# Weight chunks split three chunks ahead with four buffers, and a planner that adds a margin behind each estimated landing

## The chip, the cores and the metric

The kernel runs on one core of a Trainium2 chip. Five engines work side by side, each through its own instructions in the order in which the program lists them: TensorE (PE), VectorE (DVE), ScalarE (ACT), GpSimd (POOL) and SyncE (SP, which here only issues transfers). The metric is the device time of one execution in microseconds; the time before is the median of three runs.

## What is computed

One inference step of a one-layer decoder trunk. A prompt of 512 tokens and 8 samples of 4 tokens (32 rows) share the weights, so the projection has 544 token rows of width 2048:

```python
h = rmsnorm(x, norm_in)
z = einsum('btd,dc->btc', h, w_in)          # 7712 columns
# group A, 8 heads: sparse attention (compressed, selected, window), 2 key/value heads
# group B, 8 heads: forgetting attention, logit += D[t] - D[s], D = cumsum(log f)
mix = concat(o_n * silu(z_n), o_f * silu(z_f))
y = rmsnorm(x + einsum('btc,cd->btd', mix, w_out), norm_final)
```

The samples read 1024 past tokens each out of paged caches (8 pages of 128 rows a sample, through a page table) and a window state of 512 rows. All of it is in float32. The kernel also returns the new key/value rows, the log forget values and the shifted window state.

## The kernel before, in words

**Weights.** The input projection is 61 tiles of up to 128 columns of `w_in`, each made over four chunks of 4 x 128 rows; the first tile is made in plain float32, the other 60 tiles (240 chunks) in two parts. A raw chunk (128 x 512 floats) is fetched by SP (`raw`), then split: ACT writes its rounded high part (`whi`), DVE the rest (`wlo`). A chunk is 24 matmuls of 272 columns: two token halves, four row blocks, and for each the three products high x high, high x low, low x high (`mm3`, output `pz`). `run_tiles` goes over tiles and chunks and, in the second token half of chunk m, calls `w_split(m + W_AHEAD, part)` for the two parts; `W_AHEAD` is 2, so `whi` and `wlo` have three buffers each. `w_split` also fetches the raw chunk that lies four behind the one it splits (`w_dma`); there are five raw buffers. The finished tile is scaled into `zt` and a `post` stream stores it or hands it on.

After the last tile `run_outputs` does the same with 64 chunks of `w_out` (output `po`); `ahead(m)` keeps its splits `W_AHEAD` in front.

**Streams.** Everything else is written as Python generators, the streams: the start, the page indices, the forgetting attention (`fox`, twice sample half then prompt half, four heads each), the sparse attention (`nsa`: compression, prompt, sample), and for each of the 16 heads `mix` (gate times attention) and `turn_in` (its split into the two parts `h_hi` and `h_lo` that the output projection reads). While `run_tiles` lists the projection's matmuls, it calls `S.pump()` after every three of them, which lets every stream go on that is due, and the stream's instructions land at that place in the program.

**The planner.** When a stream is due is decided while the program is built, by the class `Clock`. It keeps an estimated time for each engine, for each transfer, and for each buffer the end of its last write and last read. A stream can yield a list of tiles: then its next step is listed once PE's planned time has passed `Clock.ready(tile)`, the latest write or read of it plus `HOP`, 0.25 us. For a tile that a transfer fills, the write's end is the estimated landing. On the chip each instruction still waits on semaphores for what it truly needs; the planner decides only the order. If a transfer lands later than planned, the instruction that needs it waits, and all that is listed behind it on its engine waits too.

The loads that streams wait on: cache pages for the forgetting attention (`fpg`, four gathers or page loads of 256 KB to a page tile, two page tiles in flight, from POOL or SP), rows for the compression (`crow`, two in flight) and its weights (`cw`), sets of cache pages for the sparse sample part (`spg`, five in flight, 48 sets), and operands that went through memory between stages (`fz`, `nz`, `fvz`, `dsb`, `kvc`; for each key/value head of the sparse prompt two keys and four query heads, one after the other; `mx` and `oz` for each mixed head, four heads at a time).

Gate tiles that are finished before the sparse sample part has given back its memory are stored (`scr_m`) and loaded later (`mx`); the later ones are written in place. The output projection can begin only when the in-projection has read `h_hi` and `h_lo` for the last time, because `turn_in` overwrites them.

**Scratch.** `dynamic_dma_scratch_size` is the memory in each partition that is set aside for the descriptors of POOL's transfers, 8192 bytes.

Of the kernel before, what the change touches and what calls it, by code (L numbers as in the profile page):

```python
# [40 lines left out]
class Clock:  # L41

    HOP = 0.25

    def __init__(self):
        self.t = dict(pe=0.0, dve=0.0, act=0.0, pool=0.0, sp=0.0)
        self.gate, self.row = {}, {}
        self.lanes = {q: [0.0] * 8 for q in ("sp", "pool")}
        self.ring, self.bus = 0.0, {}
        self.slot, self.wr, self.rd, self.plane, self.parts = {}, {}, {}, {}, {}  # L50
        self.end = 0.0
        self.stall = {}
        self.who = ""
# [14 lines left out]
        return [(*k, i) for i in range(lo // step, hi // step + 1)]  # L68

    def ready(self, ap):  # L70
        return max(max(self.wr.get(k, (0.0, 0))[0], self.rd.get(k, (0.0, 0))[0]) for k in self.keys(ap)) + self.HOP

    def packet(self, aps):
        least = 4096
# [47 lines left out]
    def note(self, eng, op, a, k):  # L122
# [12 lines left out]
        for s in reads:  # L135
            w = self.wr.get(s) if s else None
            if w:
                start = max(start, w[0] + (self.HOP if w[1] != eng else 0.0))
        for s in filter(None, writes):
            for d in (self.wr, self.rd):  # L140
                w = d.get(s)
                if w and not ("dma" in op and w[1] == "dma"):
                    start = max(start, w[0] + (self.HOP if w[1] != eng else 0.0))
        dma = "dma" in op
# [19 lines left out]
        else:  # L164
            end = start + self.cost(eng, op, outs[0], aps, accum is not None)
            self.t[eng] = end
            self.end = max(self.end, end + self.HOP)
        for s in reads:
# [152 lines left out]
def trunk_step(ctx, tc, x_prompt, x_sample, cache_nsa_kv, cache_fox_kv, cache_fox_logf, state_nsa_win,  # L321
# [4 lines left out]
    nc = Engines(tc.nc, clock)  # L326
# [71 lines left out]
    def cp(out, in_, scale=1.0):  # L398
        nc.scalar.activation(out, in_, AF.Copy, scale=scale)

    def low(hi, lo, src, scale=None):
        if scale is None:
            nc.vector.tensor_tensor(lo, src, hi, op=OP.subtract)
        else:
            nc.vector.scalar_tensor_tensor(lo, src, scale, hi, op0=OP.mult, op1=OP.subtract)
# [8 lines left out]
    def mm3(out, a, b, start, stop):  # L414
        nc.tensor.matmul(out, a[0], b[0], start=start, stop=False, skip_group_check=True)
        nc.tensor.matmul(out, a[0], b[1], start=False, stop=False, skip_group_check=True)
        nc.tensor.matmul(out, a[1], b[0], start=False, stop=stop, skip_group_check=True)

    def mm(out, a, b, start=True, stop=True):
        nc.tensor.matmul(out, a, b, start=start, stop=stop, skip_group_check=True)  # L420
# [49 lines left out]
            if ch and k % 4 == 3:  # L470
                out_steps.append((4, 4 * (ch - 1) + k // 4))
    out_steps += [(3, i) for i in range(8)]
    W_RAW, W_AHEAD = 5, 2

    def out_steps_kind(m):
        j = m - 4 * n_in
# [33 lines left out]
    def w_split(m, part):  # L510
        t, c = divmod(m, 4)
        if t == 0 or m >= 4 * n_in + len(out_steps):
            return
        n = tiles[t]["m"] if t < n_in else P
        raw = raws[m][:, :, :n]
        if part == 0:
            if t >= n_in and out_steps[m - 4 * n_in][0] == 4:
                i = out_steps[m - 4 * n_in][1]
                if "w" not in last_w:
                    wl = MX["pl"].tile([P, 2, 16, 256], F32R, name="wl", tag="mx")  # L520
                    clock.parts[wl.tensor.name] = (2 * 16 * 256, 512)
                    last_w["w"] = wl
                wsp[m] = [last_w["w"][:, x, 2 * i:2 * i + 2, :].rearrange("p a b -> p (a b)").rearrange("p (a b) -> p a b", b=P)
                          for x in range(2)]
            else:
                wsp[m] = [wts.tile([P, 4, P], F32R, name=w, bufs=W_AHEAD + 1) for w in ("whi", "wlo")]
            cp(wsp[m][0][:, :, :n], raw)
        else:
            low(*(x[:, :, :n] for x in wsp[m]), raw)
            if t < n_in:  # L530
                del raws[m]
                if m > 4:
                    w_dma(m - 1 + W_RAW)

    def run_tiles(t0, t1):
        for t in range(t0, t1):
            spec = tiles[t]
            if t == 0:
                S.need("begun")
            if t - 2 >= 0:  # L540
                S.need(f"post{t - 2}")
            n = spec["m"]
            zt = stg.tile([P, TOK], F32, name="zt", bufs=2)
            tile_of[zt.tensor.name] = t
            clock.parts[zt.tensor.name] = (TOK, HALF)
            cuts = ((0, HALF), (HALF, TOK))
            ps = [psum.tile([P, b - a], F32, name="pz", tag="pz", bufs=2) for a, b in cuts]
            raw_part = []
            for c in range(4):
                m = t * 4 + c  # L550
                if t == 0:
                    S.need(*[f"x{k}" for k in range(4 * max(c, 1), 4 * max(c, 1) + 4)])
                    for hf, cut in enumerate(cuts):
                        sl = slice(*cut)
                        for b in (h_hi, h_lo):
                            for kk in range(4):
                                mm(ps[hf][kk * 32:kk * 32 + 32], w_0["w"][:, m * 4 + kk], b[:, c * 4 + kk, sl].bitcast(F32),
                                   c == 0 and b is h_hi, c == 3 and b is h_lo)
                            S.pump()
                    w_split(m + W_AHEAD, 0)  # L560
                    w_split(m + W_AHEAD, 1)
                    if c == 3:
                        for hf, cut in enumerate(cuts):
                            cp(zt[:, slice(*cut)], ps[hf])
                        flags.add("t0")
                    S.pump()
                    continue
                hi, lo = wsp.pop(m)
                for hf, cut in enumerate(cuts):
                    sl = slice(*cut)  # L570
                    for kk in range(4):
                        k = c * 4 + kk
                        mm3(ps[hf][:n], (hi[:, kk, :n], lo[:, kk, :n]), (h_hi[:, k, sl], h_lo[:, k, sl]),
                            c == 0 and kk == 0, c == 3 and kk == 3)
                        if kk == 3 and c == 3:

                            if t > 1:
                                S.need("rsb")
                            elif t == 1:
                                raw_part.append(sl)  # L580
                            late = max(clock.t["dve"], clock.t["pe"]) > max(clock.t["act"], clock.t["pe"]) + 0.2
                            if t == 1:
                                (cp if late else nc.vector.tensor_copy)(zt[:n, sl], ps[hf][:n])
                            elif late:
                                cp(zt[:n, sl], ps[hf][:n])
                                raw_part.append(sl)
                            else:
                                nc.vector.tensor_tensor(zt[:n, sl], ps[hf][:n], rsb[:n, sl], op=OP.mult)
                        if hf == len(cuts) - 1 and kk % 2 == 0:
                            w_split(m + W_AHEAD, kk // 2)  # L590
                        if hf == len(cuts) - 1 and kk == 3 and t == n_in - 1:
                            flags.add(f"in{c}")
                        S.pump()

            def post(t=t, spec=spec, zt=zt, raw_part=raw_part):
                yield [zt]
                if t == 1:
                    yield "rsb"
                for sl in raw_part:
                    nc.vector.tensor_tensor(zt[:, sl], zt[:, sl], rsb[:, sl], op=OP.mult)  # L600
                if raw_part:
                    yield [zt]
                yield from spec["post"](zt)
                flags.add(f"post{t}")
            S.add(post(), front=True)
            S.pump()
# [197 lines left out]
    def post_kf(h):  # L804
        def f(zt):
            nc.sync.dma_start(z_scr[16 + h], zt)
            nc.vector.tensor_copy(ks_f[:, h, :], zt[:, SEQ:TOK])
            yield from store_natural(zt, *dst_fox(h, 0), False, f"k{h}")
        return f
# [1133 lines left out]
    def add_in(col, post):  # L1943
        add_tile(w_in2, [(col, P, 0)], post)
# [5 lines left out]
                 k=lambda h, _: add_in(C_KF + h * P, post_kf(h)),  # L1950
# [179 lines left out]
    if True:  # L2130
# [42 lines left out]
        for hd in range(16):  # L2173
            S.add(mix(hd))
            S.add(turn_in(hd))
        S.add(last_stage())
        run_tiles(0, n_in)
        flags.add("in_done")
        S.need("mx")
# [28 lines left out]
```

## Time and profile before

| what | value |
|---|---|
| median of three runs | 1303.0 us (1301.69 to 1304.34) |
| the profiled execution | 1298.33 us |
| its span on the core | 1296.7 us |
| granted TensorE clock, mean | 0.993 of full speed |
| moved by transfers | 265.75 MB, 205 GB/s on the mean |

Names in the profile are those of tiles: `out<-in`. All instructions go through one wrapper, line 185, so the line says nothing and the tiles say all. A group's row gives busy time, the mean length of one instruction, and the idle time of the engine before it with what ended it. A row of an engine's timeline gives start, length, engine, line, operation, tiles, and in square brackets the idle time before it and what ended that. A matmul's length in the trace includes the way through the array, so matmuls overlap: the step from start to start is the true price of one.

The stages can be told by their tiles: the start until about 30 us, compression (`crow`, `cx`) until 377, the sparse prompt (`np`) from 384 to 768, the sparse sample part (`spg`) from 772 to 1037; beside them the forgetting attention, with pages (`fpg`) from 29 to 374 and from 591 to 848; the projection runs through all of it until 1087, and the output projection from there on.

### The profile page before, as it was taken

The page shows a single profiled execution, that of the slowest core. Times are in us where ns is not written, and L with a number is a line of the kernel's source. Part 1 is how long each engine was busy: PE and PEld are TensorE (multiplying, and loading weights), DVE is VectorE, ACT ScalarE, POOL GpSimd, SP SyncE. Part 2 cuts the span into 40 slices and gives each one's busy share as a digit, 9 for nine tenths or more (in the row PEclk, how much of TensorE's full clock was granted, in tenths as well). Part 3 has the DMA queues.
Part 4 walks back from the last instruction along what each step waited for, and adds up shares of the span by engine and source line. Part 5 has one row for each costly group of instructions (what it writes and reads, how often), then busy time and mean ns, then how long its engine had stood idle before and what let it go on. Part 6 is the DMA issues. An engine that isn't in the chain of part 4 may idle for free.

```text
span 1296.7 us, 27238 instructions
## 1 busy us (share of the span) xinstructions
PE 1254.6 (97%) x10097; PEld 1131.6 (87%) x10097; DVE 786.0 (61%) x1978; ACT 546.1 (42%) x1188; POOL 284.9 (22%) x377
## 2 busy tenths in 40 slices
PE   8999999999999999998999999979899999999996
PEld 6999999988889999997999988768899898777796
DVE  5645878876546667655887745355576255345255
ACT  4413333334334667742454532236666334333221
POOL 6501466744410000004444022202111000000000
PEclk9999999999999999998999999999999999999999
DMA  8755699988986555558767579996967793334323
GB/s 211 221 132 155 211 292 295 282 255 294 315 241 157 139 168 176 147 163 292 240 206 223 155 244 251 261 268 211 260 171 206 217 328 108 101 114 156 116 76 139
DMA packets 307854, 265.75 MB, mean 205 GB/s; under 512 B 87166, under 2 KB 255118, under 8 KB 307048
## 3 DMA queue, kind: packets, MB, share of 16 engines
q1 hardware_dynamic: 283768, 188.04, 51.4%
q0 software_dynamic: 23904, 75.84, 17.8%
q8 instruction: 79, 1.29, 0.4%
q14 instruction: 55, 0.45, 0.1%
q10 hardware_dynamic: 48, 0.13, 0.0%
HBM read 235.76 MB, written 36.49 MB: 210 GB/s over the span
## 4 chain that ended last, share of the span: by engine, by line
PE 67%; DMA 12%; issue 11%; POOL 3%; DVE 3%; ACT 2%; SPq 2%; POOLq 0%; DVEq 0%; ACTq 0%
PE pz L185 38%; PE po L185 15%; PE s L185 3%; PE tr L185 3%; DMA fpg<-in_cache_fox_kv,fi 3%; DMA spg<-in_cache_nsa_kv 3%; PE accv L185 2%; POOL fpg L185 2%; PE acc L185 2%; SPq L185 2%; DMA raw<-in_w_in 2%; DMA fpg<-in_cache_fox_kv 1%; PE psb L185 1%; DMA spg<-in_state_nsa_win 1%; PE accf L185 1%
## 5 line engine op out<-in xcount | busy, mean ns | idle before, releaser
L185 PE MATMUL pz<-h_hi,whi 128*128 128x272 f32 x1920 | 566.6, 295 | 2.0 <-ACT whi L185 1.5
L185 PE MATMUL pz<-h_hi,wlo 128*128 128x272 f32 x1920 | 556.5, 290 | 10.7 <-DVE wlo L185 10.7
L185 PE MATMUL pz<-h_lo,whi 128*128 128x272 f32 x1920 | 555.4, 289 | 0.0
L185 PEld LDWEIGHTS pz<-h_hi,whi 128*128 128x128 f32 x1920 | 364.4, 190 | 20.3 <-issue 15.1
L185 PEld LDWEIGHTS pz<-h_hi,wlo 128*128 128x128 f32 x1920 | 363.8, 189 | 11.4 <-DVE wlo L185 11.4
L185 PEld LDWEIGHTS pz<-h_lo,whi 128*128 128x128 f32 x1920 | 364.3, 190 | 0.7
L185 DVE TENSOR_TENSOR wlo<-raw,whi 128x512 fp32r<-128x512 f32 x275 | 186.4, 678 | 141.5 <-ACT whi L185 136.6
L185 ACT ACTIVATE whi<-raw 128x512 fp32r<-128x512 f32 x275 | 171.8, 626 | 212.0 <-PE pz L185 107.6
L185 POOL DMA_INDIRECT fpg<-in_cache_fox_kv,fi x128 | 131.4, 1027 | 309.3 <-DMA out<-in_state_nsa_win 216.4
L185 PE MATMUL po<-whi,h_hi 128*128 128x512 f32 (+1 forms) x256 | 95.5, 373 | 0.0
L185 PE MATMUL po<-whi,h_lo 128*128 128x512 f32 (+1 forms) x256 | 93.4, 365 | 0.0
L185 PE MATMUL po<-wlo,h_hi 128*128 128x512 f32 (+1 forms) x256 | 93.4, 365 | 0.0
L185 DVE TENSOR_TENSOR zt<-pz,rsb 128x272 f32<-128x272 f32 x59 | 26.0, 440 | 110.2 <-PE pz L185 110.1
L185 POOL DMA_INDIRECT crow<-in_cache_nsa_kv,ci x64 | 66.0, 1031 | 117.7 <-DVE ct L185 78.4
L185 DVE STREAM_TRANSPOSE ft<-fpg 128x1024 f32<-128x1024 f32 x64 | 78.7, 1232 | 16.8 <-DMA fpg<-in_cache_fox_kv,fi 12.0
L185 ACT ACTIVATE cxh<-ct 128x580 fp32r<-128x580 f32 (+1 forms) x64 | 42.2, 660 | 77.9 <-DVE ct L185 69.2
L185 ACT ACTIVATE zt<-pz 128x272 f32<-128x272 f32 x63 | 25.0, 397 | 110.6 <-PE pz L185 110.3
L185 POOL DMA_DIRECT2D spg<-in_cache_nsa_kv x64 | 35.0, 546 | 163.6 <-DVE skt L185 52.4
L185 PEld LDWEIGHTS po<-whi,h_hi 128*128 128x128 f32 x256 | 48.1, 188 | 19.7 <-ACT whi L185 7.5
L185 POOL DMA_DIRECT2D fpg<-in_cache_fox_kv x64 | 35.0, 552 | 132.0 <-PE accv L185 73.9
L185 PEld LDWEIGHTS po<-whi,h_lo 128*128 128x128 f32 x256 | 48.2, 188 | 8.5
L185 PEld LDWEIGHTS po<-wlo,h_hi 128*128 128x128 f32 x256 | 48.2, 188 | 7.7
(410 smaller groups left out, 1897.9 us busy)
## 6 DMA issues: line engine op xcount, KB each, us to landing
raw<-in_w_in SPq DMA_DIRECT2D x240, 256.0 KB
fpg<-in_cache_fox_kv POOLq DMA_DIRECT2D x64, 256.0 KB, 5.9
fpg<-in_cache_fox_kv SPq DMA_DIRECT2D x64, 256.0 KB
raw<-in_w_out SPq DMA_DIRECT2D x40, 256.0 KB
spg<-in_cache_nsa_kv POOLq DMA_DIRECT2D x64, 128.0 KB, 5.0
spg<-in_cache_nsa_kv SPq DMA_DIRECT2D x64, 128.0 KB
out<-in_state_nsa_win SPq DMA_DIRECT2D x32, 254.0 KB
scr_z<-zt SPq DMA_DIRECT2D x28, 272.0 KB
```

Of the source, the lines that this page charges most:

```text
L185: return fn(*a, **k)
```

## The change

```diff
 class Clock:
 
     HOP = 0.25
+    LATE = 2.0
...
     def ready(self, ap):
-        return max(max(self.wr.get(k, (0.0, 0))[0], self.rd.get(k, (0.0, 0))[0]) for k in self.keys(ap)) + self.HOP
+        none = (0.0, 0)
+        return max(max(self.wr.get(k, none)[0] + (self.LATE if self.wr.get(k, none)[1] == "dma" and self.t["pe"] > 40.0 else 0.0),
+                       self.rd.get(k, none)[0]) for k in self.keys(ap)) + self.HOP
...
-    W_RAW, W_AHEAD = 5, 2
+    W_RAW, W_AHEAD = 5, 3
...
-                    w_split(m + W_AHEAD, 0)
-                    w_split(m + W_AHEAD, 1)
+                    for ahead in ((), (), (4,), (5, 6))[c]:
+                        w_split(ahead, 0)
+                        w_split(ahead, 1)
...
-    nc = _bacc.Bacc("TRN2", target_bir_lowering=False, num_devices=1, dynamic_dma_scratch_size=8192)
+    nc = _bacc.Bacc("TRN2", target_bir_lowering=False, num_devices=1, dynamic_dma_scratch_size=4096)
```

`W_AHEAD` of 3 splits each chunk three chunks before its use, in `run_tiles` and in `run_outputs`, and `whi` and `wlo` get four buffers each; the lines in the first tile split chunks 4, 5 and 6 there, where chunks 4 and 5 were split before. Two more buffers of 128 x 512 floats take 4096 bytes of each partition, and the scratch for POOL's descriptors is smaller by as much. `LATE` changes the planner alone: once PE's planned time is past 40 us, a stream that waits on a tile last written by a transfer goes on 2.0 us later than the estimated landing plus `HOP`. What the chip waits for is unchanged; the places of the streams' instructions in the program are not.

## Prediction

> **What bounds the kernel now.** I read the page first, then the list of PE's waits, then the timeline of each engine around the two longest ones.
>
> ```profile
> span 1296.7 us, 27238 instructions
> PE 1254.6 (97%) x10097; PEld 1131.6 (87%) x10097; DVE 786.0 (61%) x1978; ACT 546.1 (42%) x1188; POOL 284.9 (22%) x377
> ```
>
> PE (TensorE) is busy 97% of the span, every other engine far less: the time is PE's work plus PE's waits. The list of waits of PE has 19 rows; here are the first and the last, and between them those that the argument uses:
>
> ```profile
> PE pz L185 <- DVE wlo L185: 10.7, 3, 6.2
> PE pre L185 <- DMA xt<-in_x_prompt: 4.6, 5, 2.7
> PE acc L185 <- DMA spg<-in_state_nsa_win: 3.1, 1, 3.1
> PE tr L185 <- ACT sp L185: 2.5, 1, 2.5
> PE accv L185 <- DMA fpg<-in_cache_fox_kv: 1.7, 3, 0.7
> PE tr L185 <- ACT PT L185: 1.6, 1, 1.6
> PE pz L185 <- ACT whi L185: 1.5, 1, 1.5
> ...
> PE s L185 <- DMA kvc<-scr_kc: 0.6, 1, 0.6
> PE acc L185 <- DMA spg<-in_cache_nsa_kv: 0.4, 1, 0.4
> ...
> PE tr L185 <- DVE fptl L185: 0.2, 1, 0.2
> ```
>
> The columns are total, times, longest. Three kinds matter: the projection waiting for a split weight chunk (wlo, whi), a stream's matmul waiting for its transfer (spg, fpg, kvc), and transposes (tr) waiting for ACT or DVE, ten rows from 2.5 down to 0.2, some 8 us. (The xt row is the start.) What the first kind is made of, on the four engines in order of time:
>
> ```profile
> 596.24 0.61 ACT L185 ACTIVATE whi<-raw 128x512 fp32r<-128x512 f32 x1
> 601.73 1.25 DVE L185 STREAM_TRANSPOSE ft<-fpg 128x1024 f32<-128x1024 f32 x1 [6.15 <-DMA fpg<-in_cache_fox_kv,fi]
> 602.90 0.65 DVE L185 TENSOR_TENSOR wlo<-raw,whi 128x512 fp32r<-128x512 f32 x1
> 603.60 0.59 PE L185 MATMUL pz<-h_hi,wlo 128*128 128x272 f32 x1 [6.17 <-DVE wlo L185]
> ```
>
> The high part of the chunk is ready at 596.85. Its low part could follow at once, but in DVE's order a transpose of a cache page stands before it, and the page lands only at 601.7. DVE idles 6.15 us with a ready instruction behind, PE idles 6.17. The second long wait has the same build, with a page of the other cache:
>
> ```profile
> 846.44 1.25 DVE L185 STREAM_TRANSPOSE skt<-spg 128x1024 f32<-128x1024 f32 x1 [6.73 <-DMA spg<-in_cache_nsa_kv]
> 847.61 0.65 DVE L185 TENSOR_TENSOR wlo<-raw,whi 128x512 fp32r<-128x512 f32 x1
> 848.31 0.59 PE L185 MATMUL pz<-h_hi,wlo 128*128 128x272 f32 x1 [4.32 <-DVE wlo L185]
> ```
>
> So the order of the program was fixed on landings that came later than planned. The wait is not all of the price; the windows view shows what follows the waits (columns: window, length, busy us of PE, PEld, DVE, ACT, POOL, then the granted clock):
>
> ```profile
> 603.60:609.30 5.70, 5.70 (x25) 5.70 (x26) 5.66 (x10) 1.23 (x3) 2.42 (x3) 0.50 0.38 111
> 848.30:851.70 3.40, 3.39 (x15) 3.39 (x16) 3.40 (x5) 1.18 (x2) 0.00 (x0) 0.50 0.97 281
> 856.00:870.00 14.00, 11.48 (x92) 9.72 (x92) 6.77 (x21) 7.00 (x13) 0.61 (x2) 1.00 1.04 260
> 919.20:923.40 4.20, 4.20 (x25) 3.79 (x25) 0.89 (x8) 1.32 (x3) 1.10 (x2) 0.59 1.12 273
> 1037.00:1087.00 50.00, 50.00 (x402) 50.00 (x401) 28.83 (x64) 16.59 (x29) 0.00 (x0) 1.00 0.76 261
> 1087.00:1287.00 200.00, 199.92 (x1154) 157.36 (x1152) 91.43 (x189) 60.40 (x118) 0.00 (x0) 1.00 0.34 113
> ```
>
> After the idle times of 6.2, 4.3 and 3.1 us the granted clock stands at 0.50, the lower level of 1.2 GHz; around the 2.5 us wait on ACT sp (856 to 870) it stays at 1.00. At the full 2.4 GHz a 272-column matmul takes 50.00 / 402 = 0.124 us; at the lower level 5.70 / 25 = 0.228.
>
> The page of the Trainium skill "Perfetto Trace Analysis" (section Identifying the Most-Contended Engine) judges TensorE's headroom by the busy share of the weight loads. By it 1296.7 - 1131.6 = 165 us would be open. The trace disagrees: from 1087 to 1287 the loads are busy 157 of 200 us while PE is busy 199.9, so idle weight loads there are no headroom, and the sum goes by the waits.
>
> **The change part by part.** *Splitting three chunks ahead.* No instruction is added: the same 240 input and 64 output chunks are split, each one chunk earlier. A chunk is 24 matmuls, 24 x 0.124 = 3.0 us, so every whi and wlo gets 3.0 us more before PE needs it. A raw chunk is still fetched four chunks ahead of its own split, so its fetch moves along and SP's queue keeps its order of splits and fetches. With four buffers the split of chunk m+3 waits for chunk m-1, which is done when it is issued, as now. At the start one more split (0.6 us of ACT) stands ahead of the first tile's evacuation; ACT idles there longer than that:
>
> ```profile
> 29.26 0.40 ACT L185 ACTIVATE zt<-pz 128x272 f32<-128x272 f32 x1 [1.13 <-PE pz L185]
> ```
>
> So nothing; 0.6 us if that cover is gone. In the output stage PE is busy 199.9 of 200 us, so nothing there.
>
> *The margin.* A stream step that waits on a tile last written by a DMA is placed 2.0 us of planned PE time later, and so are all its instructions: DVE transposes, ACT splits, PE matmuls, and the next transfers that it issues on POOL and SP, which fall behind raw fetches that they now precede. No wait is added on the chip; an engine meets the instruction later, after more projection work. Each DMA wait in an engine's order shrinks by 2.0.
>
> *The waits.* wlo: the three rows sum to 10.7, the two long ones 6.2 and 4.3. Each gets 3.0 + 2.0 = 5.0 us, so 1.2 stays of the first and nothing of the others: 9.5 saved (if the margin changed nothing here, 3.0 + 3.0 + 0.2 = 6.2; if the splits pass the late transposes altogether, 10.7). whi: 1.5. Transfers: spg 3.1 keeps 1.1; fpg 1.7, kvc 0.6 and spg 0.4 go: 4.7. Together 15.7. PE's rows begin to count idle only after a matmul's modelled end, so each vanished wait gives back a little more: a pz matmul lasts
>
> ```profile
> L185 PE MATMUL pz<-h_hi,wlo 128*128 128x272 f32 x1920 | 556.5, 290 | 10.7 <-DVE wlo L185 10.7
> ```
>
> 290 ns against a step of 124, so 0.17 us for each of 10 waits: 1.7. Clock: 25 matmuls at 0.104 us too much are 2.6, the second stretch 15 x 0.104 = 1.6, the third 3.4 us at half speed 1.7: 5.9. Gain: 15.7 + 1.7 + 5.9 = 23.3 us.
>
> *The chains.* The streams are chains of load, wait, compute, load, and 2.0 us per exposed landing makes them longer. This costs nothing while projection work is left to fill PE. Their places:
>
> ```profile
> 427.66 0.81 SPq L185 DMA_DIRECT2D fz<-scr_z  x2
> ...
> 533.51 0.20 DVE L185 TENSOR_TENSOR npc<-npc,nsc 128x34 f32<-128x34 f32 x1
> ...
> 582.20 0.42 SPq L185 DMA_DIRECT2D nz<-out  x1
> ...
> 1005.40 0.33 SPq L185 DMA_DIRECT2D scr_o<-fot  x1
> ...
> 1037.52 49.61 PE pz L185 x396
> ```
>
> The NSA stream ends its first key/value head at 533.5 and starts the second at 582.2, when the projection has made its inputs: growth before that (four first loads 8, sixteen row gathers with two in flight 16, six loads and a constant 14: 38) falls into this gap of 48.7. After 582: six loads one by one, 12 us at most (8 if the second job pair hides two), take 10. Then its sample part: 36 waits on cache sets with five sets in flight. If only each fifth landing delays the chain, 48 / 5 x 2.0 = 19; if each wait counts, 72. I take 25, near the lower end, because DVE's list shows one such wait in the whole trace:
>
> ```profile
> DVE skt L185 <- DMA spg<-in_cache_nsa_kv: 6.7, 1, 6.7
> ```
>
> That is 35 us (27 to 84), against the last row of the fence above: 49.6 us of pure projection follow the streams' end. The forgetting-attention stream restarts at 427.7, bound by the projection, and ends at 1005.4. After 427.7 it grows by two prompt halves of 10 and one sample half of 16 to 32 for 16 two-deep key pages and 16 for eight value pairs: 52 to 68, so to 1073 at most; it isn't the later one. Then the gated heads:
>
> ```profile
> 1037.98 0.42 SPq L185 DMA_DIRECT2D mx<-scr_m  x1
> ...
> 1044.11 0.69 DVE L185 TENSOR_TENSOR mx<-mx,oz 128x512 f32<-128x512 f32 x1 [0.81 <-DMA oz<-scr_o]
> ...
> 1070.42 0.68 DVE L185 TENSOR_TENSOR mx<-mx,oz 128x512 f32<-128x512 f32 x1
> ```
>
> The first product comes 6.1 us after its load, the twelfth (this row) at 1070.4, 2.4 us apart. Load 6.1, product 0.7, a split as of a weight chunk 0.6 + 0.7 and the margin 2.0 make the first output operand ready 10 us after the streams' end: 1037.5 + 35 + 10 = 1082.5, before PE wants it at 1087. Four heads are in flight, so the margin makes a head 2.4 + 2.0 / 4 = 2.9 us, where PE takes 12 matmuls of 512 columns, 12 x 0.124 x 512 / 272 = 2.8. The lead of 4.5 us is thin, so I charge 2.
>
> *A new order.* The transposes' 8 us that no landing explains belong to the order of the program, and all of it after the first 40 us is laid out anew. They may go or double, -8 to +8; with the collisions that move I charge 3.
>
> Sum against the profiled execution: 1298.3 (span 1296.7 and 1.6 around it) - 23.3 + 2 + 3 = 1280. The median of the runs, 1303.0 (1301.7 to 1304.3), lies 4.7 above that execution; I keep this distance: 1285. A measurement tells about 0.2%, 2.6 us, from no change.
>
> **The rivals.** *The waits move.* The landings that hurt were late by 6 us, three times the margin; in a new order other pages come late with DVE's or ACT's queue behind. For it: both long waits were single events. Against: a block must now outlast some 5 us more. Price: from half of the gain (1303 - 12 = 1291) to none of it and the 3 us of collisions (1306), middle 1299. Chance 0.15.
>
> *The streams outlast the projection (slower).* One mechanism: at 1087 PE waits for the gated heads. It decides from a growth of 1087 - 1037.5 - 10 = 39 us on; I expect 35, so it is near. With 65 of the possible 84, PE idles 26 us, the clock falls behind that as above (3 us), and 23 are saved: 1303 + 26 + 3 - 23 = 1309. For it: 36 waits on sets. Against: five sets in flight and one DVE wait in the trace. Chance 0.18.
>
> *The smaller descriptor ring.* The change also halves the scratch of POOL's transfers, 8192 to 4096. In the trace POOL issues gathers without a ring wait, and each lands in 5.2 us:
>
> ```profile
> 596.56 0.95 POOL L185 DMA_INDIRECT fpg<-in_cache_fox_kv,fi  x1 [0.30 <-issue]
> ...
> fpg<-in_cache_fox_kv,fi POOLq DMA_INDIRECT x128, 5.2
> ```
>
> At 1.25 us apart four or five are in flight. If the halved ring held two, a gather would take 5.2 / 2 = 2.6 us, 1.35 more; the 64 gathers of the second half would add 86 us to the forgetting chain, beyond the projection: 1087 - 1005 - 52 leaves 30, so 56 us late: 1303 + 56 - 23 = 1336. The Trainium skill's page "Debugging Trainium Hangs" (section Descriptor Overflow) names too many descriptors for this scratch on POOL's queue as a failure; no run here shows that limit. Chance 0.04.
>
> *The margin does nothing* because late landings exceed it and the orders stay alike: only the splits count, 6.2 + 1.5 and some 1.5 of the clock: 1294. Chance 0.04.
>
> **How the numbers follow.** The forecast has 0.59: 1275 to 1297, likeliest 1285. Faster by over 2.6 us: 0.59, half of the moved waits (0.07) and the margin's failure (0.04): 0.70. Within: 0.05 of the moved waits and 0.05 of a late end that is shallow: 0.10. Slower: 0.03 of the moved waits, 0.13 of the late end, the ring's 0.04: 0.20. The range 1275 to 1305 takes in the other order's -8 and the moved waits; it leaves out the ring, the late end's deeper half, and little below.
>
> **What would show it.** In the changed profile: the wlo and whi rows of PE's waits at 2 us or less and no stretch at clock 0.50 before the end; fpg and kvc rows gone; the last stretch of pure projection shrunk from 49.6 to about 15 us, with no PE wait on h_hi or h_lo at its end; more than 11 spilled gate tiles. I am wrong if PE waits after the projection's last matmul, if POOL's issues spread beyond 1.25 us, or if new rows of the wlo kind sum to 10 us again.

## The result, and the profile after

The changed kernel takes 1295.56 us (median of 7 runs, 1292.33 to 1298.09), the kernel before on the same chip 1303.14 (7 runs, 1299.73 to 1304.74): a ratio of 0.9941, 95% interval 0.9926 to 0.9957. That is a gain of 7.6 us where 18 were forecast. Ratios here are of the fast executions of a kernel to the fast ones of the kernel before in the same session, so they can differ in the fourth digit from the ratio of the medians. The profiled execution took 1294.05 us, its span is 1292.4 at a mean granted clock of 0.983 (before: 1296.7 at 0.993): less waiting, but a lower clock.

PE's waits in the changed kernel, the whole list (total, times, longest):

```profile
PE pz L188 <- DVE zt L188: 10.1, 2, 6.7
PE tr L188 <- ACT fp L188: 6.9, 2, 6.7
PE tr L188 <- ACT sp L188: 2.5, 1, 2.5
PE pre L188 <- DMA xt<-in_x_prompt: 2.1, 1, 2.1
PE pz L188 <- DVE wlo L188: 1.8, 1, 1.8
PE tr L188 <- DVE ident L188: 1.5, 1, 1.5
PE tr L188 <- DVE ft L188: 0.7, 1, 0.7
PE accv L188 <- DVE ft L188: 0.6, 1, 0.6
PE tr L188 <- ACT np L188: 0.3, 1, 0.3
```

Every row that the forecast wanted gone is gone: wlo fell from 10.7 to 1.8, and whi, spg, fpg and kvc have no row. But the nine rows sum to 26.5 us where the nineteen of before summed to 32.3, because two new ones stand on top: the evacuation of a finished tile (`zt`, 10.1) and the transposes of the forgetting attention's weights (`fp`, 6.9). The zt rows alone reach the 10 us of new waits of the projection that the prediction had named as a sign of being wrong. The timeline (start, length, engine, tiles, then the idle time and what ended it) shows what is behind the longest of them:

```profile
845.25 1.25 DVE L188 STREAM_TRANSPOSE skt<-spg 128x1024 f32<-128x1024 f32 x1 [9.32 <-DMA spg<-in_cache_nsa_kv]
846.41 0.65 DVE L188 TENSOR_TENSOR wlo<-raw,whi 128x512 fp32r<-128x512 f32 x1
848.71 1.25 DVE L188 STREAM_TRANSPOSE skt<-spg 128x1024 f32<-128x1024 f32 x1 [1.65 <-DMA spg<-in_cache_nsa_kv]
849.88 0.40 DVE L188 TENSOR_TENSOR zt<-pz,rsb 128x272 f32<-128x272 f32 x1
850.43 0.57 PE L188 MATMUL pz<-h_hi,whi 128*128 128x272 f32 x1 [6.72 <-DVE zt L188]
```

This is the second block of the kernel before, at nearly the same time (it was at 846.4). The cache page again lands late, and DVE idles 9.3 us for it and 1.65 for the next. The split that stands between the two transposes now has lead enough and hurts nobody. The evacuation behind the second one has none: PE can't begin the next tile before its accumulator is read, and waits 6.7. The other two new waits have the same build with other names:

```profile
785.17 0.40 SPq L188 DMA_DIRECT2D raw<-in_w_in  x1
...
794.65 0.63 ACT L188 ACTIVATE whi<-raw 128x512 fp32r<-128x512 f32 x1 [9.06 <-DMA raw<-in_w_in]
795.31 0.69 DVE L188 TENSOR_TENSOR wlo<-raw,whi 128x512 fp32r<-128x512 f32 x1 [4.81 <-ACT whi L188]
795.92 0.43 DVE L188 TENSOR_TENSOR zt<-pz,rsb 128x272 f32<-128x272 f32 x1
796.41 0.59 PE L188 MATMUL pz<-h_hi,whi 128*128 128x272 f32 x1 [3.37 <-DVE zt L188]
...
971.42 0.96 SPq L188 DMA_DIRECT2D fvz<-out  x1
977.66 0.63 ACT L188 ACTIVATE fvh<-fvz 128x512 fp32r<-128x512 f32 x1 [5.99 <-DMA fvz<-out]
978.31 1.28 ACT L188 ACT_TABLE_LOAD   x1
979.60 0.51 ACT L188 ACTIVATE fp<-fp,fst 128x256 f32<-128x256 f32 x1
981.09 1.09 PE L188 MATMUL tr<-ident,fp 128*128 128x128 f32 x3 [6.68 <-ACT fp L188]
```

In the first, a raw weight chunk (the 179th issue, for the 179th split) is issued at 785.17 and split only at 794.65, when it has landed. The split itself is wanted much later, but DVE takes its low part, and the evacuation stands behind that. The issue was late too: it is listed behind the 175th split, whose low part ended at 776.6, but SP issued four loads of a stream before it, between 777.4 and 783.4. In the second, a value tile lands 6 us after its issue, ACT stands before it, and the exponentials that PE wants stand behind it, after a load of ACT's table of 1.28 us.

The transfers were busy meanwhile. These are the windows (length, busy us of PE, PEld, DVE, ACT, POOL, granted clock, transfer share, GB/s) from the issue of each of the three late loads to its landing:

```profile
785.10:794.60 9.50, 7.93 (x64) 7.71 (x62) 1.46 (x6) 0.48 (x1) 3.98 (x8) 1.00 1.03 259
833.20:845.20 12.00, 10.51 (x131) 7.78 (x129) 2.73 (x3) 2.18 (x4) 4.59 (x9) 1.00 1.10 288
971.40:977.60 6.20, 3.01 (x69) 1.64 (x53) 0.00 (x0) 0.27 (x1) 0.00 (x0) 0.86 1.10 248
```

From 760 to 1040 us the share is 0.86 on the mean.

Then the clock. The same columns for the stretches between 40 us and the end in which the granted clock is the lower level of 1.2 GHz:

```profile
600.40:603.80 3.40, 3.40 (x16) 3.40 (x16) 3.32 (x4) 0.00 (x0) 1.93 (x2) 0.50 0.66 188
794.90:801.70 6.80, 5.29 (x23) 5.29 (x24) 4.28 (x25) 1.01 (x2) 0.00 (x0) 0.50 0.70 197
846.10:856.30 10.20, 5.87 (x33) 5.84 (x41) 6.47 (x10) 0.66 (x1) 1.07 (x2) 0.50 1.07 257
866.60:870.00 3.40, 3.40 (x17) 3.40 (x16) 0.69 (x1) 1.18 (x3) 0.00 (x0) 0.50 0.95 313
975.80:986.00 10.20, 4.91 (x21) 4.69 (x22) 5.95 (x23) 7.45 (x17) 0.00 (x0) 0.50 0.39 98
```

Together 34.0 us, of which PE works 22.9 at half speed: 11.4 us lost, where the prediction priced the stretches of before at 5.9 and expected none to be left. A sixth stretch, 23.5 to 26.9 us, lies in the start, which the margin doesn't touch; it costs another 1.7. And the end, from the chain that ended last:

```profile
1044.32 38.71 PE pz L188 x309
1083.03 199.84 PE po L188 x1152
```

Of 49.6 us of pure projection behind the streams 38.7 are left, and the output projection follows without a wait. The streams end at 1044.3 us instead of 1037.5, so their chains have grown by 6.8 us, not 35; the other 4.1 are the projection's earlier end.

Where the time came from is seen best by counting. PE executes the same 10097 matmuls in each kernel, so the start of the k-th one is a yardstick (the kinds within a stretch differ by a few dozen). Us for each stretch of matmuls, from the traces; the last three columns are runs told below:

| matmuls | before | after | margin alone | margin 4.0, three ahead | margin 4.0, two ahead |
|---|---|---|---|---|---|
| 0 to 3000 | 363.7 | 361.6 | 359.4 | 360.0 | 360.9 |
| 3000 to 5000 | 259.7 | 255.2 | 259.1 | 253.7 | 254.9 |
| 5000 to 5700 | 78.7 | 78.7 | 78.7 | 80.6 | 81.5 |
| 5700 to 9000 | 397.0 | 399.6 | 398.5 | 388.4 | 381.9 |
| 9000 to the end | 197.5 | 197.3 | 197.3 | 197.5 | 197.2 |

The change gains 2.1 at the start and 4.5 around the first block (602 us), and loses 2.6 in the stretch from some 697 us on, in which the second block and the three new waits lie. That loss is hardly clear of chance: the kernel before with the smaller scratch, whose order is the same, took 398.9 us there. The gain at the start is clear: matmuls 600 to 3000 take 288.8 to 290.6 us in the four programs without a margin that ran under the same condition, and 285.0 to 286.0 in the six with one, be it of 2, 4 or 6 us.

### The profile page after: what moved, and what is told of

It reads as the page before. It is cut to its first block, busy times and chain, and to the rows that moved or that the text cites. A ratio compares the mean times of both kernels' runs of the same rounds, so it can differ in the third digit from the quotient of the medians.

```text
span 1292.4 us, 27240 instructions
## 1 busy us (share of the span) xinstructions
PE 1256.3 (97%) x10097; PEld 1138.2 (88%) x10097; DVE 786.6 (61%) x1978; ACT 548.6 (42%) x1191; POOL 287.8 (22%) x377
## 4 chain that ended last, share of the span: by engine, by line
PE 87%; DMA 6%; DVE 2%; SPq 2%; ACT 1%; issue 1%; POOL 0%; POOLq 0%; DVEq 0%; ACTq 0%
PE pz L188 51%; PE po L188 15%; PE s L188 5%; PE tr L188 5%; PE accv L188 4%; PE acc L188 3%; PE psb L188 2%; DMA raw<-in_w_in 2%; SPq L188 2%; PE accf L188 1%; DMA spg<-in_cache_nsa_kv 1%; DMA fpg<-in_cache_fox_kv 1%; DMA xt<-in_x_prompt 1%; DMA dsb<-scr_d 1%; DMA fvz<-out 0%
## 5 line engine op out<-in xcount | busy, mean ns | idle before, releaser
L188 PE MATMUL pz<-h_hi,whi 128*128 128x272 f32 x1920 | 568.3, 296 | 10.1 <-DVE zt L188 10.1
L188 POOL DMA_INDIRECT fpg<-in_cache_fox_kv,fi x128 | 134.2, 1049 | 303.3 <-DMA out<-in_state_nsa_win 208.3
L188 DVE TENSOR_TENSOR cxl<-ct,cxh 128x580 fp32r<-128x580 f32 (+1 forms) x64 | 46.1, 721 | 21.1 <-ACT cxh L188 20.8
```

Of the source, the lines that this page charges most:

```text
L188: return fn(*a, **k)
```

## The experiments

**Theories.** A: landings in this kernel come 6 to 9 us later than planned at a few places (so long an engine stands for them; the planned time itself is in no trace); a margin of 2 us leaves most of each, and the wait moves to whatever stands behind the late one in its engine's queue. B: any other order scatters by some us, and the result is one draw. C: the smaller scratch costs time. D: the landings are late because the 32 copies of the window state fill the transfer engines.

**The parts one by one.** Splits alone:

```diff
-    LATE = 2.0
+    LATE = 0.0
```

> Splits three chunks ahead with four buffers and the smaller scratch, margin 0. Theory A (late landings of 6 to 9 us block DVE and ACT; the deeper split covers only the weight chunks, a tile's evacuation behind such a landing has no lead of its own): PE's wlo and whi rows fall from 12.2 us to 6 or less, the direct DMA rows of PE (fpg, spg, kvc) stay near 5.8 us, 3 to 6 us faster than before (ratio 0.995 to 0.998). Theory B (every edit only deals the order anew; the sum of PE's waits is luck): here the streams' order is nearly that of before, so the waits stay as they are but for wlo, and the ratio is the same 0.995 to 0.998; B differs in the other runs. Theory C (the smaller scratch slows POOL's issue): POOL's spacing of 1.25 us grows and the ratio is 1.00 or more.

Measured 1300.1 us (before 1303.91), ratio 0.9976 (0.9958 to 0.9993). This is in the range of A and of B. wlo fell to 4.9, and other waits took its place:

```profile
PE accv L188 <- DMA fpg<-in_cache_fox_kv: 5.3, 7, 1.4
PE s L188 <- DVE skt L188: 5.0, 2, 4.0
PE pz L188 <- DVE wlo L188: 4.9, 1, 4.9
```

Margin alone:

```diff
-    W_RAW, W_AHEAD = 5, 3
+    W_RAW, W_AHEAD = 5, 2
-                    for ahead in ((), (), (4,), (5, 6))[c]:
+                    for ahead in ((), (), (4,), (5,))[c]:
-    ... dynamic_dma_scratch_size=4096)
+    ... dynamic_dma_scratch_size=8192)
```

> Margin 2.0 alone, splits two ahead, scratch as before. A: PE's direct DMA rows go (5.8 us to 1 or less), wlo waits of several us remain or come back where a landing is over 4 us late, so PE waits 25 to 30 us in all; ratio 0.995 to 1.000. B: any ratio from 0.990 to 1.010, with new rows of any kind.

Measured 1295.7, ratio 0.9937 (0.9916 to 0.9958): all of the change's gain, and a little more than A's range allowed. The deeper split adds nothing to it that could be measured. Its trace has the same two waits on top as the change, and a wlo of 5.4:

```profile
PE tr L188 <- ACT fp L188: 7.9, 2, 7.7
PE pz L188 <- DVE zt L188: 6.1, 1, 6.1
PE pz L188 <- DVE wlo L188: 5.4, 1, 5.4
```

The smaller scratch alone, in the kernel before:

```diff
-    ... dynamic_dma_scratch_size=8192)
+    ... dynamic_dma_scratch_size=4096)
```

> The kernel before with the scratch of 4096 alone; the order of the program is unchanged. A and B: no difference, ratio 0.998 to 1.002, POOL's gathers 1.25 us apart as before. C: gathers farther apart, ratio above 1.003.

Measured 1302.68, ratio 0.9987 (0.9970 to 1.0004), and at the first block POOL's gathers are issued 1.25 us apart as before. C falls.

**Larger margins.** The change with

```diff
-    LATE = 2.0
+    LATE = 4.0
```

> The change with a margin of 4.0 in place of 2.0. A: landings 6 to 9 us late now hold DVE and ACT 2 us less, PE's waits fall from 26.5 us to 20 or less and the stretches of lowered clock to half, 4 to 8 us faster than the change (ratio to before 0.988 to 0.991), with the last pure stretch of projection shorter than 38 us. B: no trend, ratio 0.990 to 1.000. If the chains are what costs (streams outlast the projection), slower than the change, with PE waiting on h_hi after the last pz.

Measured 1287.06, ratio 0.9880 (0.9855 to 0.9906), in A's range. The longest wait of PE is 4.1 us, and only 13.6 us before the end are at the lower clock. And with 6.0:

> The change with a margin of 6.0. Margin 2 shortened the last pure stretch of projection from 49.6 to 38.7 us, margin 4 to 18.8. A: the waits behind late landings fall further (10 us or less beside the start), but about 15 to 20 us of the stretch go once more, so the streams end with the projection: no more than 4 us gained over margin 4, or up to 10 lost if PE then waits for the gated heads (ratio to before 0.984 to 0.996). B (luck of the order): anything from 0.985 to 1.000 without that wait.

Measured 1298.34, ratio 0.9966 (0.9946 to 0.9987). Here the streams outlast the projection; PE's longest wait and the end of the chain:

```profile
PE po L188 <- ACT h_hi L188: 8.1, 1, 8.1
...
1044.86 4.16 PE pz L188 x33
1088.15 35.77 PE po L188 x157
```

The projection's last matmuls end at 1049.0 us with the streams still running: these go on until 1080, PE is busy for only 20 of the 39 us from 1049 to 1088, and the output projection then stands 8.1 us for the first operand that a gated head must deliver.

Margin 4.0 with the splits two chunks ahead and the scratch as before (the edit of margin alone, `LATE = 4.0`):

> Margin 4.0 with splits two ahead and the scratch as before. A: the margin is what acts, so within 3 us of margin 4 with splits three ahead (ratio to before 0.986 to 0.991), wlo rows of 0 to 4 us. If the deeper split is needed for a margin to act (both parts share the work): 0.992 or more, with wlo rows of 5 us and more.

Measured 1278.07 (1277.09 to 1279.4), ratio 0.9800 (0.9775 to 0.9824), the fastest version and ahead of both kernels, and faster than either sentence before the run allowed. One block of over 5 us is left, with 6.8 us at the lower clock; another 3.4 follow the 2.4 us wait on ACT's zt:

```profile
PE pz L188 <- DVE zt L188: 5.3, 1, 5.3
PE pz L188 <- DVE wlo L188: 3.3, 2, 3.0
PE pz L188 <- ACT zt L188: 2.4, 1, 2.4
...
802.90:806.30 3.40, 3.40 (x17) 3.40 (x17) 0.67 (x1) 1.91 (x2) 0.00 (x0) 0.50 0.82 284
837.00:843.80 6.80, 4.52 (x20) 4.55 (x21) 4.94 (x8) 1.18 (x2) 0.00 (x0) 0.50 1.14 260
...
1036.39 30.83 PE pz L188 x246
```

**Other cures.** The evacuations on ACT whatever the planner thinks, with the scaling later on DVE, in the change:

```diff
-                            late = max(clock.t["dve"], clock.t["pe"]) > max(clock.t["act"], clock.t["pe"]) + 0.2
+                            late = True
```

> The change (margin 2.0, splits three ahead) with every tile's evacuation on ACT and the scaling later on DVE, so that no evacuation stands behind a late page transpose on DVE. A: the two waits on DVE's zt (10.1 us) and the lowered clock behind them go, waits on ACT's zt stay small, the wait on ACT's fp may stay: 5 to 10 us faster than the change (ratio to before 0.987 to 0.991). B: other rows of the same size take their place, ratio 0.992 to 0.998.

Measured 1293.0, ratio 0.9924 (0.9900 to 0.9948), in B's range and not in A's, and not told apart from the change's 0.9941. The zt row vanishes, and again others come:

```profile
PE s L188 <- DMA kvc<-scr_kc: 4.5, 1, 4.5
PE accv L188 <- DMA fpg<-in_cache_fox_kv: 4.1, 3, 2.9
PE s L188 <- DVE nql L188: 3.6, 1, 3.6
```

So taking the evacuations out of the way moved the waits and saved no time that could be measured; that fits a late landing which costs time with anything behind it, but other landings wait in this order too. The kernel before without the 32 copies of the window state, which leaves their rows out of the output and keeps the order (the planner still counts them):

```diff
-            nc.sync.dma_start(dram(nsa_win_sample, at, [[512, 127], [1, 512]]),
-                              dram(state_nsa_win, at + 4 * 512, [[512, 127], [1, 512]]))
+            clock.note("sp", "dma_start", (dram(nsa_win_sample, at, [[512, 127], [1, 512]]),
+                                           dram(state_nsa_win, at + 4 * 512, [[512, 127], [1, 512]])), {})
```

> The kernel before without the 32 copies of the shifted window state from memory to memory (8 MB; that output's shifted rows are left out); the planner still counts them, so every other instruction stands where it stood. Theory D (landings are late because the transfer engines are full there): the first pages at 591 to 600 us land up to 6 us earlier, the wait of 6.2 us on wlo at 603 and the lowered clock behind it go, 6 to 10 us faster (ratio 0.992 to 0.995), while the waits after 770 us stay. If the gathers' own latency makes them late: the wait stays above 4 us, ratio 0.998 to 1.000.

Measured 1299.85, ratio 0.9975 (0.9956 to 0.9994). The wlo row is still 9.7 us, and DVE stands 5.5 us for the page at 602 where it stood 6.2. The transfer share there, from 594 to 602 us, is 0.99 without the copies and 1.00 with them. So most of that page's lateness is not the copies', and none of it can be at the later blocks: the last one is issued at 593.1 us (587.2 in the changed kernel). Full transfer engines without the copies are not tested by this run.

**How much is the order?** Margins beside 2.0 and 4.0, the last word of the name giving the depth of the splits:

```diff
-    LATE = 2.0
+    LATE = 1.7
```

> The change with a margin of 1.7 us instead of 2.0, everything else as changed. Where the 0.3 us less does not matter by itself, the run measures what a mere reshuffle of the order is worth. Theory A (the margin is too small against landings that are 6 to 9 us late, so 5 to 8 us of PE waits and 10 to 15 us of low clock stay, whichever buffer they fall on): 1292 to 1299, some two or three waits of over 3 us on PE, on zt, fp or wlo, at other places than in the change. Theory B (the change's time is the luck of its order): off by 6 us or more from 1295.6 on either side, below 1290 or above 1301. The forecast (margin 2 cures both long waits for good): 1285.

> The change with a margin of 2.3 us instead of 2.0. Theory A: 1290 to 1298, a little below the change since each late landing is cut by 0.3 us more, two or three waits of over 3 us stay. Theory B: off by 6 us or more from 1295.6 on either side. The forecast's mechanism (a landing 6 us late keeps 1 us of wait): 1284.

> The change with a margin of 4.3 us; beside 4.0, which gave 1287.1. Theory A (what counts is how much of the lateness the margin covers): within 4 us of it, 1283 to 1291, longest PE wait under 5 us, pure projection at the end about 15 us. Theory B (1287.1 was a lucky order): above 1292. The late end (the streams outlast the projection, which margin 6.0 showed): only if the last pure stretch, 18.8 us at 4.0, is eaten up, 1290 to 1296 with a wait of the output projection on h_hi.

> Margin 4.3 us with the splits two chunks ahead as in the kernel before (three buffers, scratch 8192); beside 4.0 with two ahead, which gave 1278.1, and the run with 4.3 and three ahead. Theory A with no use for the deeper split: 1276 to 1283 here, and 6 to 10 us below three ahead, because three ahead puts a third split (one of ACT, one of DVE) in front of the evacuations and fetches each raw chunk one chunk earlier. Theory B (1278.1 is a lucky order): above 1284, and no fixed sign against three ahead.

In these four runs and all later ones, which ran on three other chips, there was another condition: the kernel before itself took 1365.5 to 1369.2 us instead of 1303. Ratios of these runs are therefore set beside each other only, and the traces decide. Margins 1.7 and 2.3 stand in two runs each:

> Margin 1.7 us, three ahead, as in m17_three, on another chip: on the first one the kernel before itself took 1369 us instead of 1303, PE stood up to 1.8 us at a time on no tile at all between 60 and 350 us, and the ratios there say little. Theory A (waits move: two or three landings of 6 to 9 us stay uncovered wherever the order puts them): ratio 0.991 to 0.997. Theory B (luck of the order): below 0.988 or above 1.0. The forecast's mechanism: 0.986.

> Margin 2.3 us, three ahead, as in m23_three. Theory A: ratio 0.990 to 0.996, close to the change's 0.9941. Theory B: below 0.988 or above 1.0; m23_three gave 1.0122 beside m17_three's 1.0021 on a chip with other waits, which spoke for B. The forecast's mechanism: 0.985.

> Margin 3.7 us, three ahead; 4.0 gave 0.988 and 6.0 gave 0.9966 with an 8 us wait of the output projection on h_hi. Theory A (the more of the lateness is covered, the less is left, until the streams outlast the projection): 0.985 to 0.991, longest PE wait under 5 us, 15 to 25 us of pure projection left. Theory B: above 0.994 or below 0.982.

> Margin 3.7 us, splits two ahead, three buffers, scratch 8192; 4.0 with two ahead gave 0.98, and 4.3 with two ahead 0.9893 on the chip with other waits, where three ahead gave 0.9993. If the deeper split costs time at these margins by itself: 0.978 to 0.984, and 5 to 10 us below m37_three, for the third time in three. If it is the order's luck: no fixed sign against m37_three, anything from 0.98 to 0.995.

And last the change itself and the best version:

> The change as it is (2.0 us, three ahead), for the last of the scatter: its neighbours at 1.7 and 2.3 us gave 1.0006 and 1.0147 where the kernel before took 1368 us. Theory A (a margin of this size buys some 0.6% whatever the order): 0.991 to 0.998. Theory B (the order's luck decides at this size): the ratio is then one of three that span over 1.5%, and here it may be anything from 0.99 to 1.015; if the chip is the one of the first runs, 0.994.

> Margin 4.0 us, two ahead, which gave 0.980 on a chip where the kernel before took 1303 us. Theory A: below its neighbours at 3.7 and 4.3 (0.9916 and 0.9893 where the kernel before took 1368 us) or beside them, 0.980 to 0.992: the fastest version on both chips. Theory B: it was a lucky draw, above 0.993.

The third column is the stretch of matmuls 5700 to 9000 in the trace, the fourth the pure projection between the streams' last matmul and the end of the projection (before: 397.0 and 49.6).

| margin, depth | ratio to the kernel before (95%) | 5700 to 9000, us | pure projection left, us |
|---|---|---|---|
| 1.7, three | 1.0021 (0.9993 to 1.0049), 1.0006 (0.9971 to 1.0042) | 397.3, 394.6 | 33.5 |
| 2.0, three | 1.0015 (0.9990 to 1.0040) | 399.7 | 38.7 |
| 2.3, three | 1.0122 (1.0090 to 1.0153), 1.0147 (1.0106 to 1.0188) | 411.6, 412.4 | 40.6 |
| 3.7, three | 0.9877 (0.9831 to 0.9923) | 390.9 | 31.6 |
| 4.3, three | 0.9993 (0.9969 to 1.0017) | 401.1 | none: the streams end 4 us after it |
| 3.7, two | 0.9916 (0.9876 to 0.9957) | 392.2 | 33.1 |
| 4.0, two | 0.9761 (0.9722 to 0.9801) | 383.1 | 30.8 |
| 4.3, two | 0.9893 (0.9862 to 0.9924) | 392.9 | 23.7 |

What the condition looks like, the run with the change itself shows, since it is the same program as the profile after. Its matmuls 600 to 3000 take 338.9 us instead of 285.1, and PE stands there again and again for nothing that the profile shows, as do ACT and DVE; three lines from it, and its first row of PE's waits:

```profile
228.87 0.39 PE L188 MATMUL pz<-h_lo,whi 128*128 128x272 f32 x1 [1.04 <-issue]
229.58 0.59 PE L188 MATMUL pz<-h_hi,wlo 128*128 128x272 f32 x1 [0.33 <-issue]
230.26 0.39 PE L188 MATMUL pz<-h_hi,whi 128*128 128x272 f32 x1
...
PE pz L188 <- issue: 20.0, 29, 1.4
```

Here one matmul takes 0.70 us instead of 0.12, and the profile shows no operand that it waits for. Between matmuls 5700 and 9000, though, the two executions of this program agree within 0.1 us (399.6 and 399.7), those of the best version within 1.2 (381.9 and 383.1), and the repeats of 1.7 and 2.3 within 2.7 and 0.8. So that stretch can be compared across both conditions, and there the time belongs to the order of the program, not to chance from run to run.

Both theories keep a part. A's trend is there: with margins of 1.7 to 2.3 the stretch takes 395 to 412 us, with 3.7 to 4.3 it takes 382 to 393 (but for 4.3 with three ahead), with 6.0 408.6, with 397 before. B's scatter is there as well: 0.3 us of margin, from 2.0 to 2.3, moves it by 12. With 4.3 and three ahead PE waits 8.0 us for h_hi before the output projection, as with 6.0, and the stretch of 401 us holds that wait. Of the sentences written before these runs, the ratio that A named came for 3.7 with three ahead, and 4.0 with two ahead stayed the fastest when repeated. At 1.7, 2.0 and 2.3 A's ranges failed and B's held, and for 4.3 at both depths too, with three ahead with the wait on h_hi that the third sentence named. The deeper split against two ahead gave 0.9880 to 0.9800 at 4.0, 0.9993 to 0.9893 at 4.3, 0.9877 to 0.9916 at 3.7, and 0.9941 to 0.9937 at 2.0 (the first and last pair in the first condition). It is slower clear of noise in the first two pairs, one of them with the streams' late end; in the other two the intervals overlap.

## Why the prediction was right in its direction and wrong in its size

The kernel got faster, as forecast, but by 7.6 us of 18; the time of 1295.6 lies in the range that was given. Even the direction is partly luck: a margin of 2.3 made the kernel slower, and in the second condition the change itself gained nothing (1.0015).

**The weight chunks: right, and worth little.** Each wait on a split was to shrink by 3.0 + 2.0 us and 1.2 us to stay; 1.8 stayed. Alone the splits took 10.7 to 4.9, much as the 6.2 us that were worked out for them. But other rows grew, so that they gave 0.9976 alone, and nothing measurable beside the margin.

**The margin: the step that failed.** "Each DMA wait in an engine's order shrinks by 2.0", and from that the sum of 15.7 us. The order of the engines was laid out anew, and in it the engines did not wait 2 us less at each landing. DVE's rows, the first of the kernel before (its `skt` row stands in the prediction), the others of the changed one:

```profile
DVE ft L185 <- DMA fpg<-in_cache_fox_kv,fi: 12.0, 5, 6.2
...
DVE skt L188 <- DMA spg<-in_cache_nsa_kv: 11.3, 3, 9.3
DVE ft L188 <- DMA fpg<-in_cache_fox_kv,fi: 5.1, 1, 5.1
```

DVE's waits for sparse pages went from 6.7 us in one to 11.3 in three, those of the forgetting attention's from 12.0 in five to 5.1 in one. The first block was cured, by 4.4 us of PE's time (6.2 to 1.8). The second block stayed, with a longer wait of DVE (9.3 for 6.7), and two new ones came; what stood behind the late loads were instructions without lead. PE's waits fell by 32.3 - 26.5 = 5.8 us instead of 17.4 (15.7 and 1.7 for the ends that the rows hide), and 2.5 of the 5.8 are the start's xt row, which the forecast left out.

**The clock: wrong sign.** The 5.9 us that were to come back became 11.4 lost, about as large a miss as that of the waits. Counted in the same way, by whole stretches, the kernel before has three, 602.5 to 609.3, 848.3 to 851.7 and 920.0 to 923.4 us, in which PE works 12.5 us: 6.2 lost. So the clock cost 5.2 more, and 1.7 at the start. It is the number of stretches that grew: even the waits of 1.8 us (wlo) and 2.5 (sp) were followed by 3.4 us at 0.50, where in the prediction's trace the wait of 2.5 us was not. Waits and clock together give -5.8 + 5.2 + 1.7 = +1.1, where the spans differ by -4.3; the other 5.4 us lie in steps between matmuls that the waits view doesn't list, such as 2 of the 3.7 us gained between matmuls 600 and 3000, and were not traced further.

**The chains: mis-sized.** Forecast 35 us of growth, measured 6.8. The sparse sample part starts when it did (its first set of pages is issued at 772.7 us, before at 772.9), so the 10 us charged ahead of it came to nothing. From first to last set it takes 252.6 us where it took 245.0 (248.0 with the smaller scratch, in the same order): 5 to 8 us, where 25 were forecast, so less than each tenth landing delayed the chain. The rival by which the streams outlast the projection is real. It was said to decide from 39 us of growth, and the runs only bracket that: with 4.0 and three ahead 49.6 - 18.8 = 31 us of the slack were used up and PE did not wait; with 4.3 the streams ended 4 us behind the projection's last matmul, so that 53 were used up, and PE waited 8.0; with 6.0 they ended 31 us behind it.

**Collisions of the new order: mis-sized.** Charged at 3 us with ends of -8 and +8. The late stretch alone went from 15 us better (381.9) to 15 worse (412.4) than before as margin and depth changed. (The ends go back to the transposes' rows, which were read as ten with some 8 us; the list has eleven with 9.2.)

**The rivals.** "The waits move" was given 0.15 with 1291 to 1306; that is what happened, with 1295.6. The argument against it, that a block must now outlast 5 us more, was true for the splits only. The smaller ring: no effect measured. "The margin does nothing" (1294) is near in time and wrong in cause: the margin gave all of the gain in that comparison.

What stays open is why the engines stand 6 to 9 us for landings just there. Full transfer engines fit all the places: their share was 1.03 to 1.10 while the three late loads were on their way, and in the kernel before 1.01 from 596 to 602 us and 1.11 from 835 to 846.4. The share of 0.39 around 980 us belongs to the time after the landing. But no run took the load away from one of these places, so that cause isn't shown.

## What to carry to other kernels

When an instruction blocks an in-order queue because its data is late, look at everything that stands behind it, not at the one row that the wait was booked on: giving that one more lead hands the wait to the next without lead. Compare a margin in a hand-made order with the lateness that the trace shows: where engines stood 6 to 9 us for a landing, 2 us hardly helped and about 4 gave the best times. It is paid out of the slack at the end of the chains, which one row of the chain of waits gives: here 4.3 (three ahead) and 6.0 used it up. And a change that lays out the order anew should be timed at several neighbouring settings before its number is believed.

## What the runs showed of the hardware

A wait of 3.4 to 6.7 us cost another 2.5 to 3 us: the granted clock was 0.50 for 6.8 to 10.2 us around each of the three new waits, and of each PE worked 4.9 to 5.9 us at that level, half of it lost. After waits of 1.8 and 2.5 us in the same trace it was 0.50 for 3.4 us; after a wait of 2.5 us in the kernel before it stayed at 1.00.

While the loads that came late were on their way, in both kernels, the transfer share was 1.01 to 1.11, and a transfer of 256 KB (the raw chunk issued at 785.17) took 9.4 us to land.

The same program can take 1292 us or 1365: in the second condition PE, ACT and DVE stood without any releaser in the profile: 61 of the 73 us that the change's own program lost lie in its first 3000 matmuls, with steps of up to 0.70 us between matmuls that wait for nothing in the profile. The kernel before was slowed alike (1303 to 1366), and yet the ratio of the two kernels changed: the change gave 0.9941 (0.9926 to 0.9957) in the one and 1.0015 (0.9990 to 1.0040) in the other, margin 4.0 with two ahead 0.9800 (0.9775 to 0.9824) and 0.9761 (0.9722 to 0.9801). What causes it no run shows; no chip on record ran in both conditions, so it may be the chip.
